# Low parts of the weights, channel sums of the convolution and the last two operations of the attention's output: from VectorE to GpSimd

## The chip, the core and the metric

The kernel runs on one core of one Trainium2 chip. The core has TensorE (PE, matrix products and transposes, into PSUM), VectorE (DVE) and ScalarE (ACT) for elementwise work, GpSimd (POOL), and SyncE (SP), which issues the DMA transfers. Each engine works through a queue of its own in a fixed order and waits on semaphores where it needs another's result. The metric is the device time of one execution in microseconds, and lower is better.

## What is computed

One layer of a streaming encoder on x of 1 x 2048 x 1024 in float32: an input norm, then nine projections of width 1024, two parallel branches (stick-breaking attention with 16 heads of 64, and a causal depthwise convolution of 31 taps with a norm over the channels), gates, a merge, an output projection and a post-norm.

```python
def _hybrid_layer(x, w_in, w_sb_proj, conv_w, conv_b, conv_ln_g, conv_ln_b, w_cv_proj, w_out, ln_g, ln_b):
    h = x @ w_in
    q, k, v, z_sb, c_val, c_gate, z_cv, g_sb, g_cv = jnp.split(h, SPLIT_POINTS, axis=-1)
    o_sb = _stick_breaking_attention(to_heads(q), to_heads(k), to_heads(v)).reshape(bsz, seq, SB_WIDTH)
    y_sb = (o_sb * jax.nn.silu(z_sb)) @ w_sb_proj
    u = c_val * jax.nn.sigmoid(c_gate)
    u = _causal_depthwise_conv(u, conv_w, conv_b)
    u = jax.nn.silu(_layer_norm(u, conv_ln_g, conv_ln_b))
    y_cv = (u * jax.nn.silu(z_cv)) @ w_cv_proj
    merged = jax.nn.sigmoid(g_sb) * y_sb + jax.nn.sigmoid(g_cv) * y_cv
    return _layer_norm(DEEPNORM_ALPHA * x + merged @ w_out, ln_g, ln_b)

# attention: A[t,s] = sigmoid(l_ts) * prod_{s<j<t} (1 - sigmoid(l_tj)), l_ts = q_t.k_s / sqrt(Dh), s < t
```

## The kernel before

**Tiling.** The sequence is turned round in time and cut into four chunks of 512 rows (`CH`), two halves of two chunks; the 1024 channels are cut into eight blocks of 128. Every float32 product runs as three passes over an exact split of both sides into a high and a low part: high x high, high x low, low x high. `split` (line 112) makes the two parts: ScalarE writes the high part as a rounded copy (L113), VectorE subtracts it from the source (L114). L114 is a helper's line: it serves the weights (`wlo`), the activations (`xl`), the transposed attention products (`tl`) and q, k, v (`st`), which the tile names tell apart.

**Projections.** A block is 128 columns of a weight against two chunks, eight pieces of six matmuls of 512 columns (L194, into a PSUM tile `mm`, of which there are two). `load_w` (line 141) brings a block's weights in two halves of 128 x 512: a DMA into `wraw` (two buffers, L148), then `split` into `whi` and `wlo` (two buffers of a whole block each). The load of the next block stands after the second piece of the present one. There are 176 blocks.

**Attention.** For a head and 256 queries, TensorE forms logits (`lg`, L572 and L573), ScalarE takes the sigmoid (`nb`, L575), VectorE runs a product along the keys (the scan on L578, over up to 1024 columns), TensorE transposes the result (`tp`, L601), `split` makes `th` and `tl`, and TensorE multiplies with differences of v (`pv`, L617). `done` (line 626) closes a chunk of a pair of heads: L631 adds the two halves into `og`; for the second head of the pair two DMAs bring v and the gate into tiles `st`, L637 adds v, L638 multiplies with the gate, and a DMA stores `og` in DRAM as `asb`. The branch projection later reads `asb` back.

**Convolution.** `conv` (line 388) runs per block of channels and half, with 46 taps (L402) on VectorE, in two rows `y0` (in the tile `cu`) and `y1` (`cy`). Each is stored, and added to `ysum` (tile `ys`): L422 for the first block, L424 for the others. `conv_mean` multiplies `ysum` with ones on TensorE once all eight blocks of the half are in. The taps are spread out by `slow_step`, at low priority.

**Order.** TensorE's order is written out by hand: two streams, attention and projections, are woven by costs in units of TensorE time, so that what one waits for is covered by the other. The queues of the other engines and of SyncE are filled by a scheduler that places each instruction where it reckons that it can start, by priority; evictions of PSUM, `tl` and `done` have a raised priority, the taps a lowered one. Buffers of `st` (seven) rotate over all users.

Of the kernel before, what the change touches and what calls it, by code (L numbers as in the profile page):

```python
# [26 lines left out]
# The weave: buffers of weights, the lead of the logits, and distances and paces in pieces of the projection stream.  # L27
# [27 lines left out]
def layer_kernel(ctx: ExitStack, tc, x, w_in, w_sb, w_cv, w_out, vecs, cw, rows, out):  # L55
    """All sequences are reversed in time: row r is position S-1-r, so that a query r reads
    the keys s > r and the stick is broken in the direction of growing s.

    Every float32 product runs as float32r passes over an exact split a = hi + lo.

    The tensor engine runs in the order of emission: two streams, the attention and the
    projections, are woven so that what one waits for is covered by the other."""
# [29 lines left out]
    def dma(dst, src):  # L92
        """A copy of bytes: float32r has float32's bits."""
        nc.sync.dma_start(out=dst.bitcast(F32) if dst.dtype == F32R else dst,
                          in_=src.bitcast(F32) if src.dtype == F32R else src)
# [16 lines left out]
    def split(src, hi, lo):  # L112
        nc.scalar.activation(hi, src, AF.Copy)  # L113
        nc.vector.tensor_tensor(out=lo, in0=src, in1=hi.bitcast(F32), op=ALU.subtract)  # L114

    def negmean(mr):
        """-mean * rstd"""
# [22 lines left out]
    # -------------------------------------------------------------- projections, in pieces  # L140
    def load_w(src, col):
        """A block of 128 columns of a weight, [block, partition, kb, column], as hi and lo, contraction on the partitions."""
        hi = wp.tile([P, KB, P], F32R, name="whi", bufs=2)
        lo = wp.tile([P, KB, P], F32R, name="wlo", bufs=2)
        for g in range(2):
# [3 lines left out]
            split(raw, hi[:, ks], lo[:, ks])  # L149
        return hi, lo  # L150

    class Fill:
        """The pieces of the projection stream: (cost in us of the tensor engine, emit)."""
# [21 lines left out]
        def parts(self, src, col, xs, use, *by):  # L175
            """A block: the pieces, per chunk, of out^T[col.., chunk] for each (chunk, acts) of xs; use(chunk, psum, ..) takes
            it, with what the loads `by` have brought. Also the item that loads the weights of the next block."""
# [43 lines left out]
        def pair(self, one, two, first=(), freed=((), ())):  # L221
            """Two blocks, the first chunk of both before the second of either. The items `first` run beside these
            pieces, freed[n] as the activations of chunk n are used up."""
# [28 lines left out]
    def prep(c):  # L252
        """The normed input of chunk c, transposed and split, into xt[c], in pieces."""
# [721 lines left out]
```

## Time and profile before

| | |
|---|---|
| time, median of 3 runs | 3037.64 us |
| the runs | 3036.8, 3037.64, 3038.7 us |
| span of the profiled execution, first to last instruction | 3036.5 us |
| mean granted TensorE clock | 0.996 |
| DMA, mean over the span | 150 GB/s |

The time of a run contains a little around the span; the runs lie 0.3 to 2.2 us above the profiled span. Busy times are sums of an engine's instructions, so a share of 97% says that the engine has nearly always something in it, not that it is at its peak. A row of groups gives the line, the engine, the operation, the tile written and the tiles read, the shape and the count, then busy time and the mean of one in ns, then the time for which the engine stood idle just before these, and what ended it. A row of waits names who waited for whom, the total in us, how often, and the longest. A row of the timeline gives the start and the duration in us.

### The profile page before, as it was taken

What the parts mean: (1) busy time and instruction counts of PE and PEld (TensorE: products, weight loads), DVE (VectorE), ACT (ScalarE), POOL (GpSimd) and SP (SyncE); (2) the same over time, 40 slices, a digit from 0 to 9 for tenths busy, and PEclk for the clock granted to TensorE, in tenths of its full rate; (3) what the DMA queues carried; (4) which work ended last, traced back from release to release, by engine and by line L of the source; (5) the groups of instructions that cost most, each with busy time, mean ns of one, the idle gap of its engine ahead of it and who ended that gap; (6) DMA issues with size and microseconds to landing.
All of it is one profiled execution on the core that took longest, in us unless ns stands there. A gap on an engine that the chain in (4) does not pass through costs nothing.

```text
span 3036.5 us, 41850 instructions
## 1 busy us (share of the span) xinstructions
PE 2959.8 (97%) x15304; PEld 2484.1 (82%) x15304; DVE 2381.6 (78%) x3175; ACT 1269.5 (42%) x2308; POOL 88.3 (3%) x178
## 2 busy tenths in 40 slices
PE   7999999999999999999999999999999999999998
PEld 6888888888887788888888888887888878878886
DVE  5587787777879888788879888879887788856656
ACT  5333333333336344444445444445445455533222
POOL 1000000000000000000000000000000000000000
PEclk9999999999999999999999999999999999999999
DMA  7543443434434533343335344335545666685552
GB/s 269 172 144 112 148 139 117 149 125 130 139 101 140 169 100 110 114 131 123 111 112 189 103 143 141 99 103 175 164 155 161 191 224 191 208 280 197 161 189 78
DMA packets 260221, 455.92 MB, mean 150 GB/s; under 512 B 30384, under 2 KB 55088, under 8 KB 259888
## 3 DMA queue, kind: packets, MB, share of 16 engines
q1 hardware_dynamic: 260016, 453.25, 46.0%
q8 instruction: 120, 1.97, 0.3%
q14 instruction: 85, 0.70, 0.1%
HBM read 292.70 MB, written 160.43 MB: 149 GB/s over the span
## 4 chain that ended last, share of the span: by engine, by line
PE 73%; DVE 11%; issue 10%; DMA 3%; ACT 2%; POOL 1%; SPq 0%; DVEq 0%; POOLq 0%; ACTq 0%
PE mm L194 52%; PE pv L617 7%; PE tp L601 6%; DVE nb L578 3%; PE lg L573 3%; PE lg L572 3%; DVE tl L114 2%; DVE wlo L114 1%; DVE cy L402 1%; PE mo L900 1%; DMA st<-ydq 1%; DMA ydq<-st 1%; DVE xl L114 1%; DVE st L494 0%; DVE st L493 0%
## 5 line engine op out<-in xcount | busy, mean ns | idle before, releaser
L194 PE MATMUL mm<-xh,whi 128*128 128x512 f32 x2816 | 1144.5, 406 | 1.7 <-ACT whi L113 1.5
L194 PE MATMUL mm<-xh,wlo 128*128 128x512 f32 x2816 | 1110.1, 394 | 1.4 <-DVE wlo L114 1.4
L194 PE MATMUL mm<-xl,whi 128*128 128x512 f32 x2816 | 1106.2, 393 | 1.2 <-DVE xl L114 1.2
L194 PEld LDWEIGHTS mm<-xh,wlo 128*128 128x128 f32 x2816 | 530.0, 188 | 120.9 <-DVE wlo L114 1.9
L194 PEld LDWEIGHTS mm<-xl,whi 128*128 128x128 f32 x2816 | 532.9, 189 | 86.8 <-DVE xl L114 2.4
L194 PEld LDWEIGHTS mm<-xh,whi 128*128 128x128 f32 x2816 | 531.5, 189 | 86.4 <-ACT whi L113 1.9
L113 ACT ACTIVATE th<-tp 128x512 fp32r<-128x512 f32 (+1 forms) x576 | 329.4, 572 | 613.9 <-PE tp L601 606.1
L114 DVE TENSOR_TENSOR tl<-tp,th 128x512 fp32r<-128x512 f32 (+1 forms) x576 | 376.5, 654 | 180.1 <-ACT th L113 178.2
L575 ACT ACTIVATE nb<-lg 128x512 f32<-128x512 f32 (+3 forms) x640 | 334.9, 532 | 308.9 <-PE lg L573 299.0
L578 DVE TENSOR_TENSOR_SCAN nb<-nb,dd 128x256 f32<-128x256 f32 (+7 forms) x256 | 345.1, 1350 | 42.2 <-ACT nb L575 41.5
L601 PE MATMUL tp<-ident,nb 128*128 128x128 f32 x2176 | 337.8, 274 | 20.3 <-DVE nb L578 18.2
L578 DVE TENSOR_TENSOR_SCAN nb<-nb,zero 128x1024 f32<-128x1024 f32 x128 | 300.0, 2346 | 36.5 <-ACT nb L575 36.2
L601 PEld LDWEIGHTS tp<-ident,nb 128*128 128x128 f32 x2176 | 263.4, 140 | 77.9 <-DVE nb L578 22.5
L113 ACT ACTIVATE whi<-wraw 128x512 fp32r<-128x512 f32 x352 | 217.6, 629 | 261.1 <-PE mm L194 238.8
L617 PE MATMUL pv<-tl,v 128*128 128x256 f32 (+1 forms) x1152 | 292.1, 282 | 12.2 <-DVE tl L114 11.6
L114 DVE TENSOR_TENSOR wlo<-wraw,whi 128x512 fp32r<-128x512 f32 x352 | 237.4, 682 | 80.0 <-ACT whi L113 52.9
L617 PE MATMUL pv<-th,v 128*128 128x256 f32 (+1 forms) x1152 | 299.5, 281 | 0.0
L572 PE MATMUL lg<-k,qd 128*128 128x512 f32 (+3 forms) x640 | 246.4, 386 | 11.6 <-ACT nb L575 7.0
L617 PEld LDWEIGHTS pv<-tl,v 128*128 128x128 f32 x1152 | 218.1, 189 | 36.4 <-DVE tl L114 17.2
L573 PE MATMUL lg<-k,ql 128*128 128x512 f32 (+3 forms) x640 | 233.7, 366 | 0.0
L617 PEld LDWEIGHTS pv<-th,v 128*128 128x128 f32 x1152 | 217.8, 189 | 18.5 <-issue 0.2
L402 DVE SCALAR_TENSOR_TENSOR cy<-cu,csum,cy 128x512 f32<-128x512 f32 x240 | 178.1, 742 | 4.4 <-ACT cy L398 0.9
(107 smaller groups left out, 2460.0 us busy)
## 6 DMA issues: line engine op xcount, KB each, us to landing
wraw<-in_w_in SPq DMA_DIRECT2D x288, 256.0 KB, 3.2
k<-kdr SPq DMA_DIRECT2D x192, 128.0 KB, 2.9
v<-vdr SPq DMA_DIRECT2D x96, 256.0 KB, 3.5
kdr<-st SPq DMA_DIRECT2D x64, 256.0 KB, 2.1
qdr<-st SPq DMA_DIRECT2D x64, 256.0 KB, 2.2
qd<-qdr SPq DMA_DIRECT2D x128, 128.0 KB, 2.8
vdr<-st SPq DMA_DIRECT2D x64, 256.0 KB, 2.0
xr<-in_x SPq DMA_DIRECT2D x32, 256.0 KB, 3.8
```

The lines of the kernel that those rows point to most:

```text
L113: nc.scalar.activation(hi, src, AF.Copy)
L114: nc.vector.tensor_tensor(out=lo, in0=src, in1=hi.bitcast(F32), op=ALU.subtract)
L194: nc.tensor.matmul(box["ps"], lhsT=l[:, kb], rhs=r[kb], start=(kb == 0 and n == 0), stop=(kb == KB - 1 and n == 2))
L402: nc.vector.scalar_tensor_tensor(out=dst, in0=src[:, j:j + HN], scalar=t, in1=first, op0=ALU.mult, op1=ALU.add)
L572: nc.tensor.matmul(lg[:, :w], lhsT=qd[c][:, js], rhs=k2[kc][:, ko:ko + w], start=True, stop=False)
L573: nc.tensor.matmul(lg[:, :w], lhsT=ql[c][:, js], rhs=k2[kc][:, ko:ko + w], start=False, stop=True)
L575: nc.scalar.activation(nb[:, o:o + w], lg[:, :w], AF.Sigmoid, scale=-QS)
L578: nc.vector.tensor_tensor_scan(out=nb[:, :w], data0=nb[:, :w], data1=dd[:, :w] if diag else zero.to_broadcast([P, w]), initial=0.0 if diag ...
L601: nc.tensor.transpose(out=tp[:, at_:at_ + P], in_=tiles[j][:, so:so + P], identity=ident)
L617: nc.tensor.matmul(o[:, :w], lhsT=lv, rhs=tt[:, o0:o0 + w], start=(diag and t == 0 and n == 0 and e == 0), stop=(last and t == nt - 1 and ...
L900: nc.tensor.matmul(ps, lhsT=a[kb][:, js], rhs=b[:, kb, qs], start=(kb == 0 and n == 0), stop=(kb == KB - 1 and n == 2))
```

## The change

`split` takes an engine for the low part, VectorE where none is given; `load_w` gives it GpSimd, so that `wlo` is formed there. The four `ysum` operations of each block of channels move to GpSimd (L422, L424), as do L637 and L638 in `done`. The high parts, all other splits, the DMAs and all shapes stay. The rest of the file's differences are comments and docstrings that are taken out; line numbers don't move.

```diff
-    def split(src, hi, lo):
+    def split(src, hi, lo, eng=None):
         nc.scalar.activation(hi, src, AF.Copy)
-        nc.vector.tensor_tensor(out=lo, in0=src, in1=hi.bitcast(F32), op=ALU.subtract)
+        (eng or nc.vector).tensor_tensor(out=lo, in0=src, in1=hi.bitcast(F32), op=ALU.subtract)
...
             raw = wp.tile([P, 4, P], F32, name="wraw", bufs=2)
             nc.sync.dma_start(out=raw, in_=src[col // P][:, ks])
-            split(raw, hi[:, ks], lo[:, ks])
+            split(raw, hi[:, ks], lo[:, ks], nc.gpsimd)
...
             for e, y in enumerate((y0, y1)):
                 dma(ydr[h, m][:, e], y)
                 if m == 0:
-                    nc.vector.tensor_copy(out=ysum[h][:, e], in_=y)
+                    nc.gpsimd.tensor_copy(out=ysum[h][:, e], in_=y)
                 else:
-                    nc.vector.tensor_tensor(out=ysum[h][:, e], in0=ysum[h][:, e], in1=y, op=ALU.add)
+                    nc.gpsimd.tensor_tensor(out=ysum[h][:, e], in0=ysum[h][:, e], in1=y, op=ALU.add)
                 yield
...
-            nc.vector.tensor_tensor(out=g, in0=g, in1=v, op=ALU.add)
-            nc.vector.tensor_tensor(out=g, in0=g, in1=z, op=ALU.mult)
+            nc.gpsimd.tensor_tensor(out=g, in0=g, in1=v, op=ALU.add)
+            nc.gpsimd.tensor_tensor(out=g, in0=g, in1=z, op=ALU.mult)
             dma(asb[c, i], g)
```

TensorE's order stays the same, instruction for instruction. On VectorE, GpSimd and SyncE the scheduler places the work anew. VectorE first, in the second half of the attention: the scans (L578, listed here as SCALAR_TENSOR_TENSOR on `nb`) over 768 and 640 columns of one step, before.

```order
L114 TENSOR_TENSOR tl<-tp,th 128x512
L114 TENSOR_TENSOR wlo<-wraw,whi 128x512
L344 TENSOR_TENSOR st<-mm,st 128x512
L578 SCALAR_TENSOR_TENSOR nb<-nb,dd 128x768
L114 TENSOR_TENSOR wlo<-wraw,whi 128x512
L402 SCALAR_TENSOR_TENSOR cy<-cu,csum,cy 128x512
L114 TENSOR_TENSOR tl<-tp,th 128x512
L402 SCALAR_TENSOR_TENSOR cy<-cu,csum,cy 128x512
L114 TENSOR_TENSOR tl<-tp,th 128x512
L578 SCALAR_TENSOR_TENSOR nb<-nb,dd 128x640
```

The same place on VectorE now:

```order
L114 TENSOR_TENSOR tl<-tp,th 128x512
L344 TENSOR_TENSOR st<-mm,st 128x512
L578 SCALAR_TENSOR_TENSOR nb<-nb,dd 128x768
L402 SCALAR_TENSOR_TENSOR cy<-cu,csum,cy 128x512
L114 TENSOR_TENSOR tl<-tp,th 128x512
L402 SCALAR_TENSOR_TENSOR cy<-cu,csum,cy 128x512
L114 TENSOR_TENSOR tl<-tp,th 128x512
L578 SCALAR_TENSOR_TENSOR nb<-nb,dd 128x640
```

Both `wlo` are gone from between the scans and the `tl`; the rest stands as it stood. GpSimd's queue in the same part of the program, where one operation on a column (L324, on `vnext`) followed the last with nothing between, before:

```order
L324 TENSOR_TENSOR st<-vnext,st 128x1
L373 COPY cu<-halo 128x2x15
L324 TENSOR_TENSOR st<-vnext,st 128x1
L326 COPY vnext<-st 128x1
L324 TENSOR_TENSOR st<-vnext,st 128x1
```

And now, from one such pair to the next:

```order
L324 TENSOR_TENSOR st<-vnext,st 128x1
L114 TENSOR_TENSOR wlo<-wraw,whi 128x512 x3
L637 TENSOR_TENSOR og<-og,st 128x512
L638 TENSOR_TENSOR og<-og,st 128x512
L114 TENSOR_TENSOR wlo<-wraw,whi 128x512 x6
L637 TENSOR_TENSOR og<-og,st 128x512
L638 TENSOR_TENSOR og<-og,st 128x512
L114 TENSOR_TENSOR wlo<-wraw,whi 128x512 x2
L124 TENSOR_TENSOR var<-var,mhalf 128x4
L114 TENSOR_TENSOR wlo<-wraw,whi 128x512 x2
L424 TENSOR_TENSOR ys<-ys,cu 128x512
L114 TENSOR_TENSOR wlo<-wraw,whi 128x512 x4
```

The low parts, the channel sums and the attention's last two operations now stand in one queue, in which each waits for the one ahead. On SyncE the loads of raw weights (L148) wait for a `wlo` on GpSimd now; the order there is changed in places, mostly by one row or two.

## Prediction

> **What bounds the kernel now.** I read the page's first two parts, then the waits of TensorE by stage, then the VectorE groups that the change moves.
>
> ```profile
> PE 2959.8 (97%) x15304; PEld 2484.1 (82%) x15304; DVE 2381.6 (78%) x3175; ACT 1269.5 (42%) x2308; POOL 88.3 (3%) x178
> ...
> PE   7999999999999999999999999999999999999998
> ```
>
> TensorE (PE) is busy 97% of the span, at nine tenths or more in all slices but the first and the last. Its idle time is 3036.5 - 2959.8 = 76.7 us, and that is the most that any change away from TensorE can win. VectorE (DVE) is busy 78%, GpSimd (POOL) 3%. The change takes work from the second and gives it to the third, so what counts is the part of the 76.7 us in which TensorE waits for VectorE, and whether that part shrinks. The next fence has the busy time by stage (first number the stage's length, then each engine), then TensorE's larger waits for VectorE in the same three stages, in us, times and longest.
>
> ```profile
> 40.00:940.00 900.00, 892.79 (x4532) 748.48 (x4531) 681.72 (x961) 339.39 (x650) 34.97 (x63) 1.00 0.43 140
> 940.00:2200.00 1260.00, 1235.24 (x6656) 1043.43 (x6655) 1059.91 (x1332) 563.21 (x1049) 22.24 (x34) 1.00 0.40 130
> 2200.00:2660.00 460.00, 442.83 (x2425) 376.35 (x2426) 382.62 (x476) 230.51 (x419) 2.03 (x2) 0.99 0.59 188
> ...
> PE tp L331 <- DVE st L320: 1.1, 1, 1.1
> ...
> PE pv L617 <- DVE tl L114: 7.8, 8, 1.9
> PE tp L601 <- DVE nb L578: 5.8, 7, 1.8
> ...
> PE tp L601 <- DVE tl L114: 1.9, 5, 0.6
> PE tp L331 <- DVE st L320: 1.8, 1, 1.8
> ...
> PE tp L601 <- DVE nb L578: 12.3, 7, 3.2
> PE pv L617 <- DVE tl L114: 3.9, 5, 1.4
> ```
>
> The third number is VectorE's load: 681.72 / 900 = 75.7%, 1059.91 / 1260 = 84.1% and 382.62 / 460 = 83.2%. The waits are 1.1 us (0.12% of the stage), then 7.8 + 5.8 + 1.9 + 1.8 = 17.3 us (1.37%), then 12.3 + 3.9 = 16.2 us (3.5%). Two things follow. The prize is about **34.6 us**, 1.1% of the kernel. And it is all but absent where VectorE is at 76% and there where it is at 83 to 84%, so a few points of VectorE's load matter. This is how such a wait looks:
>
> ```profile
> 1282.73 0.66 DVE L114 TENSOR_TENSOR wlo<-wraw,whi 128x512 fp32r<-128x512 f32 x1
> ...
> 1283.31 0.74 DVE L402 SCALAR_TENSOR_TENSOR cy<-cu,csum,cy 128x512 f32<-128x512 f32 x1
> ...
> 1283.97 0.68 DVE L114 TENSOR_TENSOR tl<-tp,th 128x512 fp32r<-128x512 f32 x1
> ...
> 1284.71 0.38 PE L617 MATMUL pv<-tl,v 128*128 128x256 f32 x1 [1.90 <-DVE tl L114]
> ```
>
> TensorE stood 1.90 us for a `tl` that stood on VectorE behind a weight's low part (`wlo`) and a tap of the convolution. Without the `wlo` it is some 0.6 us earlier.
>
> **What is taken off VectorE.** Groups of VectorE by shape: busy time, mean ns of one, then its idle time before them.
>
> ```profile
> L114 DVE TENSOR_TENSOR wlo<-wraw,whi 128x512 fp32r<-128x512 f32 x352 | 237.4, 682 | 80.0 <-ACT whi L113 52.9 <-PE tp L601 17.7 <-PE lg L573 7.9
> L637 DVE TENSOR_TENSOR og<-og,st 128x512 f32<-128x512 f32 x32 | 22.0, 686 | 17.5 <-DMA st<-vtd 17.4
> L638 DVE TENSOR_TENSOR og<-og,st 128x512 f32<-128x512 f32 x32 | 21.8, 680 | 1.7 <-DMA st<-gat_5b 0.7 <-DMA st<-gat_3b 0.5 <-DMA st<-gat_4b 0.2
> L424 DVE TENSOR_TENSOR ys<-ys,cy 128x512 f32<-128x512 f32 x14 | 9.5, 679 | 0.0
> L424 DVE TENSOR_TENSOR ys<-ys,cu 128x512 f32<-128x512 f32 x14 | 9.5, 678 | 0.0
> ```
>
> That is 237.4 + 22.0 + 21.8 + 9.5 + 9.5 = **300.2 us** in 444 instructions, 12.6% of VectorE's busy time (the four copies that begin a sum are left out as too small). Up to 80.0 + 17.5 + 1.7 = 99 us go too in which VectorE stood at the head of its queue for ScalarE's `whi` or for a load. I don't count them: what stood behind may not have been ready either.
>
> **What GpSimd pays.** No row shows a two-input operation of this size there. The nearest are a memset of twice the columns and a two-input operation on one column (fastest, median, slowest):
>
> ```profile
> L506 POOL MEMSET dd<- 128x1024 f32 x1 | 1.0, 952 | 0.0
> ...
> L324 POOL TENSOR_TENSOR st<-vnext,st x24: 191/692/1798, 63.3 to 2010.3; 128x1 f32<-128x1 f32 x24
> ```
>
> One pass over 512 columns is 0.952 / 2 = 0.48 us, the fixed part 0.19 us. One pass gives 0.67 us, three passes (two reads and a write in turn) 1.63 us; I take two reads in turn, 0.19 + 0.95 = 1.14 us, between them. 444 x 1.14 = 506 us (297 to 724), so GpSimd goes from 3% to about 20%. It isn't short of time. The Trainium skill (GPSIMD Engine Reference, Elementwise — side-by-side cycle accounting) puts such an operation at about 2.6 cycles an element at 1.2 GHz, from which an estimate is 1.11 us and a sum of 493 us; no run here shows it.
>
> Does a slower low part make TensorE wait? The 352 halves are 176 blocks in 3036.5 us, 17.3 us each. A block's weights are loaded when two of the eight pieces of the block before are through, so six eighths of a block, 12.9 us, cover the load, `whi` and `wlo`. GpSimd's 0.5 us more for each half lies under that, and so do a few us of waiting in its queue. The present cover shows in the one wait, at 2679 us:
>
> ```profile
> PE mm L194 <- DVE wlo L114: 1.4, 1, 1.4
> ...
> SPq L148 <- DVE wlo L114: 458.9, 232, 14.8
> ```
>
> There the attention ends, its last sums (L637, L638) go to the store and come back at once, and they now stand in GpSimd's queue ahead of urgent low parts: I add 2 us (0 to 5). The second row is the other queue: SyncE (SP) issues the load of the next raw weights as soon as the low part has freed the buffer, and stands there 232 times; what is queued behind it (stores that free the seven `st` buffers, loads of keys) is later by what the low part is later. These have leads of several us, so I put it at 1 us, from 0 to 10.
>
> **What the two engines do to each other.** This decides it. GpSimd's few operations are stretched at times; each pair below is a GpSimd row and what VectorE ran beside it.
>
> ```profile
> 1544.58 2.21 POOL L373 COPY cu<-halo 128x30 f32<-128x30 f32 x1 [2.40 <-DVE ys L424]
> ...
> 1544.44 2.34 DVE L578 TENSOR_TENSOR_SCAN nb<-nb,zero 128x1024 f32<-128x1024 f32 x1
> 1546.70 0.66 DVE L424 TENSOR_TENSOR ys<-ys,cy 128x512 f32<-128x512 f32 x1
> ...
> 342.73 1.50 POOL L322 TENSOR_SCALAR st<-st 128x1 f32<-128x1 f32 x1 [77.17 <-DMA ql<-qdr]
> ...
> 342.93 0.68 DVE L320 TENSOR_TENSOR st<-st 128x511 f32<-128x511 f32 x1
> 343.53 0.68 DVE L578 TENSOR_TENSOR_SCAN nb<-nb,dd 128x256 f32<-128x256 f32 x1
> ...
> 121.81 0.18 POOL L326 COPY vnext<-st 128x1 f32<-128x1 f32 x1
> ...
> 121.62 0.68 DVE L114 TENSOR_TENSOR tl<-tp,th 128x512 fp32r<-128x512 f32 x1
> ```
>
> A copy of 30 columns took 2.21 us and ended at 1546.79, as the scan beside it did (1546.78). An operation on one column took 1.50 us and ended at 344.23, after two VectorE operations back to back (the last ended at 344.21). Beside `tl`, which has one input in PSUM, a copy took 0.18 us. So GpSimd stands while VectorE runs an operation with both inputs in SBUF. The Trainium skill (SBUF — State Buffer, SBUF: two separate sides) says that the two share a port pair as an exclusive lock, that a VectorE operation with two SBUF inputs takes it against a GpSimd operation that reads SBUF, and that whichever starts first keeps it for the whole instruction. The trace agrees for GpSimd's side; that VectorE stands for GpSimd, no row shows, since GpSimd's operations here were too short.
>
> By what part of its time VectorE is exposed:
>
> ```profile
> L578 DVE TENSOR_TENSOR_SCAN nb<-nb,dd 128x256 f32<-128x256 f32 (+7 forms) x256 | 345.1, 1350 | 42.2 <-ACT nb L575 41.5
> ...
> L578 DVE TENSOR_TENSOR_SCAN nb<-nb,zero 128x1024 f32<-128x1024 f32 x128 | 300.0, 2346 | 36.5 <-ACT nb L575 36.2
> ...
> L402 DVE SCALAR_TENSOR_TENSOR cy<-cu,csum,cy 128x512 f32<-128x512 f32 x240 | 178.1, 742 | 4.4 <-ACT cy L398 0.9 <-issue 0.3
> L402 DVE SCALAR_TENSOR_TENSOR cu<-cd,cwt,cu 128x512 f32<-128x512 f32 x240 | 178.1, 742 | 2.7
> L402 DVE SCALAR_TENSOR_TENSOR cy<-cu,cwt,cy 128x512 f32<-128x512 f32 x240 | 178.0, 742 | 2.3
> ```
>
> Scans and taps alone are 300.0 + 345.1 + 3 x 178.1 = 1179 us, half of VectorE's busy time, all with both inputs in SBUF. If GpSimd holds off VectorE in turn, each of the 444 operations costs VectorE between nothing and the whole 1.14 us. About half the time the next VectorE operation is of the exposed kind; then it waits 1.14 us if it is next at once, and 1.14 - 0.68 = 0.46 us if a `tl` of 0.68 us lies between. Half and half, that is 0.5 x 0.8 = 0.40 us each, **178 us** in all (0 to 506).
>
> **The sum.** VectorE: -300 + 178 = -122 us, 5.1% of its time, or 4.3 points of load in the two late stages. By the line through the first and second stage (1.25 points of waiting for 8.4 of load) the second loses 0.64% of 1260 us, 8 us; by that through the first and third (3.4 for 7.5) the third loses 1.9% of 460 us, 9 us: 17 us together. A more cautious count: the 34.6 us are some 34 waits; with 4 us of queue ahead of each, 5.1% of it is 0.2 us, 7 us together. I take 11 us, between the two, and give back 2 us at 2679 us and 1 us on SP's queue: **-8 us**. The span of 3036.5 us becomes 3028.5; the runs of before lie 0.3 to 2.2 us above the span and their median 1.1, so the forecast is **3030 us**, 0.25% below the 3037.6.
>
> Ends: with nothing held off, VectorE loses 12.6% of its load and all 34.6 us go, 3003. With 1.14 us each, VectorE gains 506 - 300 = 206 us, 8.6% or 7 points: the same lines give +14, +15 and +9 us in the three stages, 3037.6 + 38 = 3076.
>
> **Rivals.** (1) *VectorE stands for GpSimd, and longer than it is relieved.* One mechanism: a GpSimd operation holds off scan or tap, the `tl` and `nb` behind it come late, TensorE stands. It turns the sign once the mean hold is above 300 / 444 = 0.68 us; at 0.9 us the load rises by 100 us, 3.5 points, and the lines give +18 us, 3056; at the end above 3076. For it: half of VectorE's time is of the exposed kind, and in the rows above GpSimd enters as soon as such an operation ends. Against: VectorE's next operation began at 1546.70, before the scan's end, without a gap for the copy's sake. The Trainium skill (Perfetto Trace Analysis, Optimizing Scalar/DVE Operations) warns that the shared port may make a move between these two worthless. 24%.
> (2) *No change.* The waits for `nb` (5.8 + 12.3 us) mostly follow a scan of 2.35 us that had only just got its input; taking work from ahead of it helps little, and GpSimd's holds give the rest back: 3037, from 3032 to 3043. For it: in the example only 0.66 of the last 2.1 us ahead of the matmul are moved. 30%.
> (3) *The change moves the work, but its lateness is what counts*: SP stands longer at the raw weights' loads, the `st` buffers come free late, and the evictions of `mm` hold TensorE. 352 loads later by 1 us with a tenth of it uncovered are 35 us, less the 11 us gained: 3062. Against: TensorE waited for low parts once. 4%.
> The forecast, faster: 42%.
>
> **How the numbers follow.** Faster by over 0.2% (6 us, about what a measurement of this kernel can tell from no change) is the forecast's 42%; within it is rival 2's 30%; slower is 24% and 4%. Both signs hold much of it, so: the forecast's own range is 3008 to 3031, and the range for 8 in 10 is 3010 to 3068, which leaves out the last of the full relief and the worst of the holds.
>
> **What would show it.** Right: VectorE at about 2080 us less its stretched operations, GpSimd near 600 us or more, TensorE's waits for `tl` and `nb` below 34.6 us, none for `wlo` outside 2660 to 2690 us. Rival 1 shows as taps above 742 ns and scans above 2346 ns, and more waits for `tl` and `nb`; rival 3 as waits for `wlo` and longer waits of SP at L148. A GpSimd mean above 2 us, or TensorE's waits for VectorE unchanged with VectorE's load well down, would make the forecast wrong.

## The result: slower by 1.5%, and the profile after

The changed kernel takes **3083.5 us** (median of 4 runs, 3081.8 to 3084.7) against 3038.2 us before (3036.8 to 3039.1): a ratio of 1.0148, 95% interval 1.0133 to 1.0162. The prediction said 3030, with a range up to 3068. The profiled execution's span went from 3036.5 to 3081.1 us, 44.6 us more. First the page's busy times after:

```profile
PE 2976.3 (97%) x15304; PEld 2491.8 (81%) x15304; DVE 2314.3 (75%) x2727; ACT 1271.1 (41%) x2308; POOL 766.2 (25%) x626
```

VectorE (DVE) did get lighter, from 2381.6 to 2314.3 us and from 78 to 75% of its time. TensorE (PE) still stands longer: 3081.1 - 2976.3 = 104.8 us idle, against 76.7. It is also 16.5 us longer busy with the same 15304 instructions. The same three stages as in the prediction (the stage's length, then each engine's busy time, then TensorE's granted clock), and below them, stage by stage, what TensorE waited for:

```profile
40.00:940.00 900.00, 889.03 (x4504) 744.32 (x4502) 648.64 (x788) 336.68 (x644) 273.83 (x228) 1.00 0.42 138
940.00:2200.00 1260.00, 1223.98 (x6547) 1032.50 (x6547) 1017.54 (x1132) 557.56 (x1034) 313.02 (x219) 0.99 0.39 126
2200.00:2660.00 460.00, 433.44 (x2364) 366.30 (x2363) 365.41 (x400) 224.76 (x412) 85.37 (x57) 0.99 0.57 184
```

```profile
PE tp L331 <- DVE st L320: 1.9, 1, 1.9
PE tp L601 <- DVE tl L114: 1.6, 2, 1.3
PE tp L601 <- DVE nb L578: 1.1, 2, 0.9
...
PE tp L601 <- DVE nb L578: 11.9, 8, 3.5
PE pv L617 <- DVE tl L114: 9.5, 11, 1.9
...
PE tp L601 <- DVE tl L114: 4.9, 5, 1.8
...
PE tp L601 <- DVE nb L578: 10.5, 6, 3.6
PE pv L617 <- DVE tl L114: 9.8, 10, 2.3
```

VectorE's load is 648.64 / 900 = 72.1%, 1017.54 / 1260 = 80.8% and 365.41 / 460 = 79.4%: in every stage three to four points below before. The waits shown are 4.6 us, 26.3 us and 20.3 us, where before had 1.1, 17.3 and 16.2. So load and waits went in opposite directions. Over the whole span TensorE's waits of more than 0.15 us grew by 20.3 us for VectorE, by 5.7 us for ScalarE and by 1.6 us for GpSimd, nearly all of the 28.1 us of idle time. The groups show what became of the operations (busy time, mean ns of one, idle time before):

```profile
L578 DVE TENSOR_TENSOR_SCAN nb<-nb,zero 128x1024 f32<-128x1024 f32 x128 | 311.6, 2437 | 45.3 <-ACT nb L575 45.0
L402 DVE SCALAR_TENSOR_TENSOR cy<-cu,cwt,cy 128x512 f32<-128x512 f32 x240 | 209.0, 871 | 2.2
L402 DVE SCALAR_TENSOR_TENSOR cu<-cd,cwt,cu 128x512 f32<-128x512 f32 x240 | 206.7, 861 | 2.8
...
L701 DVE TENSOR_TENSOR st<-mm,gt 128x512 f32<-128x512 f32 x64 | 43.9, 686 | 84.0 <-PE mm L194 78.4 <-DMA gt<-gat_3s 5.2
L631 DVE TENSOR_TENSOR og<-pv,st 64x512 f32<-64x512 f32 x64 | 43.8, 685 | 25.3 <-ACT st L630 24.1
...
L638 POOL TENSOR_TENSOR og<-og,st 128x512 f32<-128x512 f32 x32 | 59.0, 1843 | 2.4 <-PE mm L194 0.2
...
L637 POOL TENSOR_TENSOR og<-og,st 128x512 f32<-128x512 f32 x32 | 47.7, 1492 | 232.7 <-DMA st<-vtd 155.3 <-DVE og L631 49.8 <-DVE bs L262 13.6
```

The taps (L402) went from 742 to 861 and 871 ns, the scans on 1024 columns from 2346 to 2437. L701 and L631, which have one input in PSUM, kept their 686 and 685 ns (the same two figures before). GpSimd's own times for a low part (count: fastest, median, slowest ns):

```profile
L114 POOL TENSOR_TENSOR wlo<-wraw,whi x352: 1265/1299/3278, 13.2 to 2961.8; 128x512 fp32r<-128x512 f32 x176
```

So an undisturbed low part takes 1.27 to 1.30 us there. The slow ones are those in which GpSimd stood for VectorE: of the 122 above 1.45 us, 117 began while a VectorE operation with no input in PSUM was running, of the other 230 only 25. The other direction shows as plainly: after the first 40 us, 245 VectorE operations took over 0.15 us longer than the median of their like before, and within 0.1 us of the start of every one of them a GpSimd operation was running, though GpSimd is busy only a quarter of the time. One place shows how this reaches TensorE. The timeline of the kernel after, rows of GpSimd, VectorE and TensorE (start us, duration us; in brackets the wait):

```profile
1645.57 2.97 POOL L114 TENSOR_TENSOR wlo<-wraw,whi 128x512 fp32r<-128x512 f32 x2 [13.45 <-ACT whi L113]
...
1645.64 1.77 DVE L494 TENSOR_TENSOR st<-st 128x512 f32<-128x512 f32 x1
1647.34 3.08 DVE L578 TENSOR_TENSOR_SCAN nb<-nb,dd 128x896 f32<-128x896 f32 x1
...
1650.47 0.44 PE L601 MATMUL tp<-ident,nb 128*128 128x128 f32 x2 [3.50 <-DVE nb L578]
```

Two low parts ran from 1645.57 to 1648.54. L494 began beside the first and took 1.77 us in place of the 0.70 that is its mean before; the scan behind it took 3.08 in place of a mean of 2.02. That is 1.07 + 1.06 = 2.1 us of the 3.5 for which TensorE then stood. What followed is seen in the same kernel's windows around that place (length, busy TensorE, weight loads, VectorE, ScalarE, GpSimd, then TensorE's granted clock):

```profile
1646.00:1651.00 5.00, 1.50 (x11) 1.19 (x10) 5.00 (x3) 1.47 (x3) 2.54 (x2) 1.00 0.70 236
1651.00:1653.00 2.00, 0.99 (x5) 0.67 (x4) 1.96 (x5) 0.00 (x0) 0.00 (x0) 0.64 0.95 344
1653.00:1658.00 5.00, 5.00 (x16) 4.03 (x16) 4.25 (x6) 2.98 (x5) 0.00 (x0) 0.50 0.07 26
1658.00:1662.00 4.00, 4.00 (x22) 3.42 (x21) 2.38 (x5) 2.44 (x5) 0.00 (x0) 0.95 0.31 103
```

After the wait TensorE worked for some 6.8 us at a clock of 0.50, so a wait of 4.5 us (3.50 and another of 1.00) cost 3.4 us more. Over the whole kernel, the span and mean granted clock of before and of after:

```profile
core 0: 3036.5 us, clock 0.996
```

```profile
core 0: 3081.1 us, clock 0.992
```

The clock took 0.4% of 3036.5 = 12 us before and 0.8% of 3081.1 = 25 us after. Idle time (+28.1 us) and clock (+12.5 us) together make 40.6 of the 44.6 us. In windows of 1 us over the whole span I count six stretches of half clock before and eleven after. The last of each lies at the kernel's end, where TensorE has no more work; the other five and ten take 1.7 or 3.4 us each, about 12 us more after than before.

### The profile page after: what moved, and what is told of

The parts are those of the page before. It is cut to its first block, busy times and chain, and to the rows that moved or that the text cites. A ratio compares the mean times of both kernels' runs of the same rounds, so it can differ in the third digit from the quotient of the medians.

```text
span 3081.1 us, 41942 instructions
## 1 busy us (share of the span) xinstructions
PE 2976.3 (97%) x15304; PEld 2491.8 (81%) x15304; DVE 2314.3 (75%) x2727; ACT 1271.1 (41%) x2308; POOL 766.2 (25%) x626
## 5 line engine op out<-in xcount | busy, mean ns | idle before, releaser
L114 POOL TENSOR_TENSOR wlo<-wraw,whi 128x512 fp32r<-128x512 f32 x352 | 530.4, 1517 | 1605.0 <-ACT whi L113 1466.9
L578 DVE TENSOR_TENSOR_SCAN nb<-nb,dd 128x256 f32<-128x256 f32 (+7 forms) x256 | 376.6, 1474 | 61.2 <-ACT nb L575 60.6
L578 DVE TENSOR_TENSOR_SCAN nb<-nb,zero 128x1024 f32<-128x1024 f32 x128 | 311.6, 2437 | 45.3 <-ACT nb L575 45.0
L402 DVE SCALAR_TENSOR_TENSOR cy<-cu,csum,cy 128x512 f32<-128x512 f32 x240 | 204.8, 853 | 11.3 <-ACT cy L398 7.5
```

Source lines behind the costliest of these rows:

```text
L114: (eng or nc.vector).tensor_tensor(out=lo, in0=src, in1=hi.bitcast(F32), op=ALU.subtract)
L402: nc.vector.scalar_tensor_tensor(out=dst, in0=src[:, j:j + HN], scalar=t, in1=first, op0=ALU.mult, op1=ALU.add)
L578: nc.vector.tensor_tensor_scan(out=nb[:, :w], data0=nb[:, :w], data1=dd[:, :w] if diag else zero.to_broadcast([P, w]), initial=0.0 if diag ...
```

## The experiments

Fourteen kernels, each timed in three rounds (d_ys_og_only in five) beside the kernel before on the same chip. **Hold** below is how much longer VectorE was busy than it would be by its own work alone. For that, a_relief gives the measure: 444 operations less took 2381.6 - 2128.6 = 253 us off VectorE, 0.57 us each, not the 0.68 of a single row, since rows of VectorE overlap a little. **Price** is the time lost per us of hold, against before or against a_relief, whichever has the same work on VectorE. Ratios are turned into us with before's 3038.2.

| kernel | what it is | ratio to before, 95% | VectorE busy | hold | price |
|---|---|---|---|---|---|
| after | the change | 1.0148 [1.0133, 1.0162] | 2314.3 | 186 | 0.32 |
| a_relief | moved work left out | 0.9953 [0.9938, 0.9968] | 2128.6 | 0 | |
| b_price | before, and GpSimd does the moved work again | 1.0427 [1.0408, 1.0447] | 2651.9 | 270 | 0.48 |
| c_wlo_only | low parts alone moved | 1.0124 [1.0100, 1.0147] | 2334.4 | 153 | 0.32 |
| d_ys_og_only | the other 96 operations alone moved | 1.0042 [1.0030, 1.0055] | 2371.7 | 45 | 0.35 |
| e_memset | before, 704 memsets on GpSimd | 1.0002 [0.9993, 1.0011] | 2384.1 | 3 | |
| f_twice_dve | before, VectorE does the moved work again | 1.0161 [1.0147, 1.0175] | 2635.5 | 254 (own work) | 0.19 |
| l_dup_first | f with the added low parts put first | 1.0175 [1.0158, 1.0192] | 2637.8 | 256 (own work) | 0.21 |
| g_cut4 | after, low parts in four pieces | 1.0165 [1.0151, 1.0179] | 2234.3 | 106 | 0.61 |
| i_one_input | before, GpSimd operations with one input | 1.0141 [1.0125, 1.0156] | 2444.9 | 63 | 0.68 |
| j_free512 | before, 352 GpSimd operations nobody waits for | 1.0218 [1.0201, 1.0235] | 2557.5 | 176 | 0.38 |
| k_free128 | the same in 1408 short pieces | 1.0105 [1.0090, 1.0120] | 2469.7 | 88 | 0.36 |
| n_relief_hold | a_relief, 352 operations nobody waits for, one tile read twice | 1.0050 [1.0035, 1.0065] | 2227.3 | 99 | 0.30 |
| p_two_tiles | the same, two tiles read | 1.0087 [1.0072, 1.0102] | 2279.5 | 151 | 0.27 |
| q_from_raw | the same, on the raw weights | 1.0101 [1.0084, 1.0117] | 2280.8 | 152 | 0.30 |

(c and d: by 0.57 us for each moved operation; their own relief is added to the loss at a_relief's rate.) The theories at first: (1) VectorE is held off by GpSimd's operations; (2) the scheduler's new order costs; (3) what GpSimd now makes comes late.

### What the move takes away, and what it brings

a_relief: the kernel without the moved work, in the order of VectorE that this leaves.

```diff
-        lo = wp.tile([P, KB, P], F32R, name="wlo", bufs=2)
+        lo = wzero
...
-            split(raw, hi[:, ks], lo[:, ks])
+            nc.scalar.activation(hi[:, ks], raw, AF.Copy)
...
-                else:
-                    nc.vector.tensor_tensor(out=ysum[h][:, e], in0=ysum[h][:, e], in1=y, op=ALU.add)
...
-            nc.vector.tensor_tensor(out=g, in0=g, in1=v, op=ALU.add)
-            nc.vector.tensor_tensor(out=g, in0=g, in1=z, op=ALU.mult)
```

> The relief alone: the moved work is done nowhere. All low parts of the weights are one constant tile of zeros, the channel sums keep only their first block, and the attention's last two operations are left out (so the output lacks these); GpSimd has no more to do than before. Theory 1 (VectorE is held off by GpSimd's operations): nothing is held off, and VectorE's load falls by 12.6%; by the prediction's line the waits of 34.6 us in front of TensorE go, 3003 us, by its cautious count 3022 us; so 3000 to 3025 us, taps at 742 ns. Theory 2 (the scheduler's new order on VectorE and ScalarE is what costs): this kernel has nearly the same new order, so it is slow too, 3060 to 3085 us. Theory 3 (the low parts come late from GpSimd): as theory 1 here.

It took 3027.2 us, by the ratio 14 us less than before and 2 us above the range of theory 1; the taps stayed at 742 ns. Its page and its waits of TensorE:

```profile
PE 2960.0 (98%) x15304; PEld 2485.1 (82%) x15304; DVE 2128.6 (70%) x2731; ACT 1268.7 (42%) x2308; POOL 81.3 (3%) x179
```

```profile
PE tp L602 <- DVE nb L579: 14.0, 10, 2.5
...
PE pv L618 <- DVE tl L114: 7.4, 13, 1.4
```

Without the moved work TensorE still waits 14.0 us for scans and 7.4 us for `tl`. The relief was never worth 34.6 us. And 2677 of its 2731 VectorE instructions follow one another as in the kernel after: an order close to the new one isn't slow by itself, so theory 2 falls: from here to the kernel after it is 59 us the other way.

b_price: VectorE as before; GpSimd does the same operations once more, in place on buffers that are used up.

```diff
             split(raw, hi[:, ks], lo[:, ks])
+            nc.gpsimd.tensor_tensor(out=raw, in0=raw, in1=hi[:, ks].bitcast(F32), op=ALU.subtract)
...
+                nc.gpsimd.tensor_tensor(out=d0[:, :HN], in0=y, in1=y, op=ALU.add)
...
+            nc.gpsimd.tensor_tensor(out=v, in0=v, in1=z, op=ALU.add)
+            nc.gpsimd.tensor_tensor(out=z, in0=v, in1=z, op=ALU.mult)
```

> The price alone: VectorE does all that it did before, in the order of before, and GpSimd does an operation of the same size and kind beside each of the 448 moved ones, a second time, into buffers that are already read, so that nobody waits for its results except for the buffers. Theory 1: VectorE is held off as in the changed kernel, its taps take 850 to 870 ns in place of 742, and with nothing taken off VectorE the time is above that of the changed kernel, 3085 to 3130 us. Theory 2: the order is that of before, so 3035 to 3045 us. Theory 3: nothing waits for a low part from GpSimd, so 3035 to 3050 us.

3173.5 us, above the 3085 to 3130 of theory 1, with the taps at 861 ns, as expected. VectorE is 270 us longer busy with the same 3175 instructions, 0.60 us for each of the 448 operations. GpSimd's work costs VectorE time, whoever uses the result.

c_wlo_only: the change without L424, L637 and L638.

```diff
-            split(raw, hi[:, ks], lo[:, ks])
+            split(raw, hi[:, ks], lo[:, ks], nc.gpsimd)
```

> Only the low parts of the weights on GpSimd, the channel sums and the attention's last two operations on VectorE: 352 of the 448 operations. Theory 1: the price goes by the number of GpSimd's operations, 352 / 448 of the 45 us, so 3065 to 3080 us. Theory 2: anything between 3038 and 3083 us. Theory 3: the low parts are those that come late, so the whole of it, 3075 to 3085 us.

3080.6 us: most of the loss comes with the low parts. The time lies in the range of theory 3 and 0.6 us above that of theory 1, so this run doesn't tell hold from lateness.

d_ys_og_only: the rest of the change alone (the edit is the change's at L422, L424, L637 and L638).

> The change without the low parts: only the channel sums and the last two operations of the attention's output (96 operations) on GpSimd, the low parts on VectorE. With the price in proportion to the number of operations, by the kernel after (448 operations, +45 us): +10 us, 3050 us. By the difference of after (3083) and c_wlo_only (3081, low parts only): +3 us, 3043 us. If these 96 operations had stood ahead of awaited VectorE results in before: below 3036 us. Theory 3 (lateness) would show as SyncE standing longer for og and TensorE waiting for the loads behind it: 3045 us or more.

3052.6 us, +13 us, near the 10 us in proportion to the number of operations. The 96 operations cost about what the low parts cost, each. The time also lies in the range of theory 3, and its signs are there in part: SyncE stands 114.3 us for `og` in place of 76.8, and TensorE's wait for `whi` behind a load rose from 1.5 to 4.2 us (p_two_tiles below, where nothing waits for GpSimd's results, has 4.2 us as well). TensorE's waits for VectorE rose by only 2.7 us. For these 96 operations the run doesn't part hold from lateness.

e_memset: as before, and GpSimd writes the raw weights' buffer after its last reader.

```diff
             split(raw, hi[:, ks], lo[:, ks])
+            for _ in range(2):
+                nc.gpsimd.memset(raw, 0.0)
```

> All as before on VectorE, and GpSimd writes zeros twice over each raw weight buffer after it was used (704 memsets of 128x512, about 0.5 us each, so as much of GpSimd's time as the low parts take by one pass less). They read nothing. Theory 1 in the form that GpSimd's reading of SBUF is what holds VectorE off: taps stay at 742 ns, 3035 to 3045 us (the buffer is free about 1 us later). Theory 1 in the form that any GpSimd access holds it off: taps at 800 ns or more and 3060 us or more. Theories 2 and 3: 3035 to 3045 us.

3040.5 us, no difference. The taps of VectorE and the memsets in it:

```profile
L404 DVE SCALAR_TENSOR_TENSOR cy<-cu,csum,cy 128x512 f32<-128x512 f32 x240 | 178.3, 743 | 4.6 <-ACT cy L400 0.9 <-issue 0.3
...
L151 POOL MEMSET wraw<- 128x512 f32 x704 | 368.7, 527 | 2025.7 <-DVE wlo L114 1933.8 <-issue 21.0 <-ACT nb L577 15.8
```

A GpSimd that writes 128x512 704 times leaves the taps at 743 ns: it must read SBUF to hold VectorE off. These memsets also free the raw buffer about 1.05 us later, which costs nothing.

### Load or hold

Two further theories: (A) TensorE's waits follow VectorE's load, however it came about; (B) it counts where the time is lost. f_twice_dve is b_price with the added operations on VectorE itself.

```diff
             split(raw, hi[:, ks], lo[:, ks])
+            nc.vector.tensor_tensor(out=raw, in0=raw, in1=hi[:, ks].bitcast(F32), op=ALU.subtract)
...
+                nc.vector.tensor_tensor(out=d0[:, :HN], in0=y, in1=y, op=ALU.add)
...
+            nc.vector.tensor_tensor(out=v, in0=v, in1=z, op=ALU.add)
+            nc.vector.tensor_tensor(out=z, in0=v, in1=z, op=ALU.mult)
```

> The kernel before, with the work that b_price gave to GpSimd a second time (352 low parts, the channel sums, the last two operations of the attention's output) done that second time on VectorE instead. It adds about 300 us of busy time to VectorE, a little more than the 270 us by which GpSimd's operations lengthened VectorE's in b_price (3173 us). Theory A (TensorE's waits follow VectorE's total load, however the load came about): as slow as b_price or slower, 3165 to 3210 us. Theory B (what counts is where the time is lost: the scheduler puts added VectorE operations where nothing urgent stands behind them, a hold by GpSimd falls ahead of any operation): clearly below b_price, 3060 to 3120 us.

```profile
PE 2976.3 (96%) x15304; PEld 2491.5 (81%) x15304; DVE 2635.5 (85%) x3623; ACT 1269.1 (41%) x2308; POOL 85.3 (3%) x178
```

3088.4 us. VectorE is at 85%, and the kernel is about as slow as the one after with VectorE at 75%. The same work a second time costs 49 us on VectorE and 130 us on GpSimd. Theory A falls.

l_dup_first gives f's added low parts priority:

```diff
+            with tc.high_priority(offset=500):
+                nc.vector.tensor_tensor(out=raw, in0=raw, in1=hi[:, ks].bitcast(F32), op=ALU.subtract)
```

> f_twice_dve (the moved work done a second time on VectorE, 3088 us) with the 352 added low parts at a high priority, so that 216 of VectorE's 3623 rows stand elsewhere: an added low part stands directly ahead of a tl or nb 144 times in place of 115, directly ahead of a scan 73 times or so in place of 37 to 40. The work is the same. If place decides (theory B): 3095 to 3130 us, towards the price of a hold. If only the amount counts (theory A): 3083 to 3093 us.

3093.1 us; its interval overlaps f's. So the place shows no price here, but the test was a weak one: in the traces 144 of the 352 added low parts stand directly ahead of a scan or a `tl`, in place of 115. Theory B is neither shown nor refuted by 29 of them, and what sets a hold apart from work stays open.

### Length of the operations, and inputs

g_cut4:

```diff
-            split(raw, hi[:, ks], lo[:, ks], nc.gpsimd)
+            nc.scalar.activation(hi[:, ks], raw, AF.Copy)
+            for j in range(4):
+                nc.gpsimd.tensor_tensor(out=lo[:, g * 4 + j], in0=raw[:, j], in1=hi[:, g * 4 + j].bitcast(F32), op=ALU.subtract)
```

> The kernel after, with each low part on GpSimd cut into 4 operations of 128 columns (1408 for 352). If a hold of VectorE lasts as long as the GpSimd operation that makes it and its length counts (theory B): each hold is at most about 0.4 us in place of 1.3 us, and the time falls from 3083 to 3040 to 3065 us; taps that were held show +0.4 us, not +1 us. If only the total of GpSimd's time on SBUF counts (theory A): 4 fixed parts for one raise GpSimd's total, so 3083 to 3110 us. If lateness of the low parts counted (theory 3): slower than 3083 us as well, with TensorE waiting for wlo.

3089.8 us, no gain, in the range for GpSimd's total time and not in that for the length, though the hold fell from 186 to 106 us. One reason shows in its waits of TensorE:

```profile
PE tp L333 <- POOL st L326: 4.2, 4, 2.4
```

GpSimd is at 37% there, and its small urgent operations stand behind the pieces. But this row is a small part of the loss. Beside the kernel after, TensorE's waits for VectorE did fall, from 70.1 to 59.7 us, while those for ScalarE rose from 17.6 to 23.2 us and those for GpSimd from 1.6 to 4.9 us, and TensorE was 8.9 us longer busy with the same instructions. Why ScalarE comes later is not explained.

i_one_input, on GpSimd:

```diff
+            nc.gpsimd.tensor_scalar(out=raw, in0=raw, scalar1=2.0, scalar2=None, op0=ALU.mult)
...
+                nc.gpsimd.tensor_scalar(out=d0[:, :HN], in0=y, scalar1=2.0, scalar2=None, op0=ALU.mult)
...
+            nc.gpsimd.tensor_scalar(out=v, in0=v, scalar1=2.0, scalar2=None, op0=ALU.mult)
+            nc.gpsimd.tensor_scalar(out=z, in0=z, scalar1=2.0, scalar2=None, op0=ALU.mult)
```

> The kernel before and, on GpSimd, 448 operations of 128x512 with ONE input in SBUF and an output in SBUF (a multiplication by 2 in place on the raw weights, and on buffers of the convolution and the attention's output that are used up), in the places of b_price's two-input operations. If any GpSimd operation that reads SBUF holds VectorE off: taps at 780 to 850 ns in place of 743, time 3060 to 3173 us. If it takes two inputs on GpSimd's side: taps at 743 ns and time 3040 us, as with the memsets. Per unit of GpSimd's time the same hold as in b_price (270 us for 717 us) would make the ratio of VectorE's gain to GpSimd's gain 0.38 again.

3083.1 us, the taps at 768 to 776 ns: one input read from SBUF is enough for a hold, though a smaller one (63 us). That is 0.08 us for each of the 789 us that GpSimd gained, where b_price's 0.38 was expected, and the taps lie below the expected 780 to 850 ns; why is open. Its price of 0.68 is out of line. As in b_price, the raw buffer comes free only after VectorE's low part and then GpSimd's operation; what of the two prices is due to that was not separated.

j_free512 and k_free128 take that away: nothing waits for their operations.

```diff
+    scr = wp.tile([P, 4, P], mybir.dt.bfloat16, name="scr", bufs=1)
...
+            nc.gpsimd.tensor_tensor(out=scr, in0=hi[:, ks].bitcast(F32), in1=hi[:, ks].bitcast(F32), op=ALU.add)
```

k_free128 has four such operations of 128 columns, into a float32 tile.

> The kernel before, untouched on VectorE, and on GpSimd 352 operations of 128x512 with two inputs in SBUF, which read a weight's high part twice and write a scratch tile that nothing reads. Nothing waits for them (the high part is kept for a whole block anyway), so neither the weight's loads nor any result of the kernel come later. If the hold of VectorE alone makes the loss: VectorE's busy time rises by 180 to 230 us (352 operations at 0.52 to 0.60 us, the means of the kernel after and of b_price), and the time by 80 to 110 us, 352/448 of b_price's 133 us: 3120 to 3150 us. If b_price's loss came from the raw weights' buffers being free later: 3040 to 3060 us.

> The same with 1408 operations of 128x128 in place of 352 of 128x512 (0.45 us each alone in g_cut4, against 1.27 us), nothing waiting for them. If the length of a single hold counts more than their sum: VectorE's busy time +100 to +150 us, the time clearly below that of the run with 352 operations, 3060 to 3090 us, and so g_cut4's lack of a gain was the lateness of GpSimd's small operations behind a busier queue. If the time goes with GpSimd's time on SBUF: 1408 x 0.45 = 634 us against 352 x 1.27 = 447 us, so slower than the run with 352 operations, by up to 40%.

3106.0 us, below the expected 3120 to 3150, and 3070.8 us, as expected. A hold that delays nothing else costs 0.38 and 0.36 us per us; in j_free512 VectorE's 3175 instructions stand in the very order of before. Where the hold falls is not as in the change, though: about half of j_free512's, 89 us, lies on VectorE's own low parts (682 ns before), which start beside GpSimd's operation.

```profile
L114 DVE TENSOR_TENSOR wlo<-wraw,whi 128x512 fp32r<-128x512 f32 x352 | 326.7, 936 | 69.9 <-ACT whi L113 57.5 <-PE tp L604 4.7 <-DMA k<-kdr 3.8
```

Short operations hold VectorE off less in all (88 us against 176), though GpSimd's own busy time is longer. So for the hold, four short operations beat a long one; g_cut4 lost that again.

### Hold or lateness

The last question was whether the hold alone makes the loss, or late low parts and late weight buffers do. Three kernels on top of a_relief (the moved work is left out in all): n_relief_hold reads the high part twice, p_two_tiles the zero tile and the high part, q_from_raw the raw weights and the high part.

```diff
+            nc.gpsimd.tensor_tensor(out=scr, in0=hi[:, ks].bitcast(F32), in1=hi[:, ks].bitcast(F32), op=ALU.add)
...
+            nc.gpsimd.tensor_tensor(out=scr, in0=wzero[:, ks].bitcast(F32), in1=hi[:, ks].bitcast(F32), op=ALU.subtract)
...
+            nc.gpsimd.tensor_tensor(out=scr, in0=raw, in1=hi[:, ks].bitcast(F32), op=ALU.subtract)
```

> The kernel a_relief (the moved operations done nowhere: low parts a constant zero tile, channel sums of the first block alone, the last two operations of the attention's output left out; 3027 us) and on GpSimd 352 operations of 128x512 that read a weight's high part twice and write a scratch tile that nothing reads: the hold of the change's low parts without any result that could come late. If hold and relief make the whole result: VectorE's busy time 170 to 200 us above a_relief's 2129, time 3065 to 3085 us, as in c_wlo_only (3081). If half or more of the loss was that low parts or weight buffers come later: 3035 to 3055 us.

n_relief_hold's 3053.2 us lie in the range for lateness, but it doesn't decide: its operations were shorter (median 1042 ns) and held VectorE off for 99 us, not 170 to 200.

```profile
L150 POOL TENSOR_TENSOR scr<-whi x352: 1035/1042/2904, 14.2 to 2934.9; 128x512 f32<-128x512 f32 x176
```

> n_relief_hold with two different tiles as GpSimd's operands (the constant zero tile and the weight's high part, into a scratch tile), so that an operation should take the 1.27 to 1.30 us of the change's low parts and not 1.04; as in a_relief the moved operations are done nowhere. Nothing waits for it. At 0.30 us of time for each us of hold (the kernel after against a_relief: 56 us for 186): if the hold of VectorE comes back to 170 to 190 us, 3075 to 3085 us, and the hold alone makes the loss. If the hold is back and the time stays at 3050 to 3060 us, the rest is lateness. If the hold stays near 100 us, the operations' length is not what set it, and 3050 to 3060 us.

> The same with the raw weights and the high part as GpSimd's operands, the change's own, into a scratch tile: the raw weights' buffer comes free as late as in the kernel after, no low part is waited for (they are a constant zero tile; the other moved operations are left out, as in a_relief). If the hold alone counts: as p_two_tiles, within 5 us, and 3075 to 3085 us. If the raw buffer's lateness counts: 15 us or more above p_two_tiles. If the low part's own lateness counts: more than 15 us below c_wlo_only's 3081 us.

```profile
L150 POOL TENSOR_TENSOR scr<-wlo,whi x352: 1261/1299/3145, 14.0 to 2946.9; 128x512 f32<-128x512 f32 x176
```

```profile
PE 2969.6 (97%) x15304; PEld 2489.2 (81%) x15304; DVE 2279.5 (74%) x2731; ACT 1268.5 (41%) x2308; POOL 606.4 (20%) x531
```

With the change's own 1.30 us, the hold is 151 and 152 us and the times are 3066.7 and 3070.8 us, 8 and 4 us below the lower end of what I expected, with a hold that is 20 to 40 us smaller than expected. By the ratios p_two_tiles lies 41 us above a_relief and q_from_raw 45 us. The 4 us between them are what a late raw buffer could cost; the intervals overlap. Add the other 96 operations, d_ys_og_only's 13 us and the 3 us that their relief would have brought at a_relief's rate: 45 + 13 + 3 = 61 us, and the kernel after lies 59 us above a_relief. So the hold explains the result, within intervals of some 5 us either way for each of these times; low parts that come late have no share that these runs can show. Of the 59 us, 45 are shown with nothing but the hold and a late raw buffer; for the 16 us of the other 96 operations, lateness of `og` isn't ruled out.

No kernel here that computes the same is faster than the one before. a_relief's 14 us are what taking this work off VectorE brought with nothing put elsewhere, and no run found a place for it that costs less.

## Why the prediction was wrong

**What held.** TensorE is the bound and the sign hangs on what GpSimd does to VectorE: so it was. *"If GpSimd holds off VectorE in turn"*: it does. The hold was put at 0.40 us for each operation, 178 us in all; it was 186 us for 448, 0.41 each. Half of 444 operations were to hold VectorE off by 0.8 us, and 245 VectorE operations were stretched, by 0.80 us in the mean. That it came so close is in part luck: for operations of the same size it was 0.28 us each in n_relief_hold and 0.60 us in b_price. The signs named for rival 1 all came, slower taps and scans and more waits for `tl` and `nb`. The rule on the shared port that the prediction took from the Trainium skill (SBUF — State Buffer, SBUF: two separate sides) is now seen from the other side too: taps are stretched from 742 to 861 ns and more, scans of 1024 columns from 2346 to 2437, `tl` with its PSUM input keeps its mean of 654, and beside memsets the taps stay at 743. Lateness of low parts was put at 2 us; TensorE waited once, 0.5 us. GpSimd's price was put at 1.14 us and is 1.27 to 1.30 alone and 1.52 in the mean; the estimate from the Trainium skill (GPSIMD Engine Reference, Elementwise — side-by-side cycle accounting), 1.11 us, was as low. Neither matters to the time, since GpSimd has room.

**The step that failed** is in the sum: *"VectorE: -300 + 178 = -122 us"*, turned into waits *"by the line through the first and second stage"*. It takes a us of hold as equal to a us of VectorE's work and lets waits follow the load. Both terms were priced wrong.

1. The relief. VectorE's busy time fell by 253 us without the moved work, not by 300.2 (rows overlap), and all of it brought 14 us, where the lines of load gave the whole 34.6: 14 / 253 = 0.06 us per us. The prediction's own cautious count comes close when it is applied to the full relief: 34 waits, 4 us of queue ahead of each, 10.6% of it, 14 us.
2. The hold. 186 us cost 59 us, 0.32 each, five times as much; in kernels where nothing waits for GpSimd it was 0.27 to 0.38. So -14 + 59 = **+45 us**, what was measured. (The 59 us are taken from the same two times; what checks them is the 61 us from p_two_tiles, q_from_raw and d_ys_og_only.) VectorE's net load does fall, by 67 us, and tells nothing.
3. The clock. Every term of the sum counted waits alone. About 12 of the 45 us are TensorE at half clock after a long wait.

The lines of load aren't far off for work that is added on VectorE itself: f_twice_dve's 254 us are 10.7% of its load, 46 us by these lines, and 49 us were measured. About a third of those 49 is TensorE's longer busy time at the lower clock (16.5 us), which the lines leave out, so this nearness is partly luck too. What the lines miss is that the relief brings less than half of what they give it, and that a hold isn't work. (At the prediction's upper end the 14, 15 and 9 us belong to the second, third and first stage; their sum stands.)

**Rival 1** had the mechanism and the place, with 24%, but by the same sum its turning point was a mean hold of 0.68 us. With the measured prices it is 14 us / (448 x 0.32) = 0.10 us: 0.41 is far beyond it. That such time is dear and the relief cheap was not in any row of before.

**Why a hold is dearer than work** is shown in part. In the traces I counted, after 40 us, TensorE's waits of 0.4 us or more for VectorE, and VectorE operations over 0.15 us longer than the median of their like before. In the kernel after, 245 operations are stretched, by 0.8 us in the mean and 1.15 at most. Of 40 waits (54.6 us), 32 (44.8 us) have more than 0.5 us of stretch in operations that ended within the 6 us before the wait's end; a random moment has that in 33% of cases. The other 8 waits make 9.8 us. Before, there were 28 waits with 34.2 us, and a_relief has 18 with 20.8 us. So relief does take away waits, and holds make more of them. Why VectorE's own added work costs less than a hold, 0.19 to 0.21 us per us against 0.27 to 0.38, stays open: l_dup_first moved too few operations to tell whether it is their place in the order. That a hold comes when GpSimd happens to be ready, and no order can be made for it, is my guess and was not tried.

## What to carry to other kernels

When work is moved to an engine whose operations may hold off those of the one it left, price the two directions apart: what the relieved engine's work costs the bound engine (leave the work out and look), and what the other engine's operations cost while nothing waits for them. Busy time of an engine off the critical path is no measure for either: here it fell and the kernel lost 45 us. And where the bound is TensorE, add to each wait of about two us or more the half clock that may follow it.

## What the runs showed of the hardware

- **TensorE's clock after a wait.** Stretches at 0.50 last about 3.4 or 6.8 us and follow waits from about 1.8 us on, though not all: a wait of 2.26 us at 2503 us in the kernel after was followed by one, one of 2.97 us at 2646 us was not. b_price has nineteen of them and a mean clock of 0.985. The Trainium skill (TensorE: Matmul & The Clock Gate, Part 1: The HAM clock gate) tells of a free-running window of about 3.4 us and half clock after an idle one; the lengths agree, and the traces add that a wait shorter than the window can be enough.
- **GpSimd's operations of 128x512.** Two tiles 1.30 us, the same tile twice 1.04, one tile times a number 1.50, and 128 columns of two tiles 0.46 (medians). From 1.30 and 0.46: 2.2 ns a column and 0.18 us fixed. By the prediction's count of passes over SBUF one input would have been cheaper than two.
- **A short GpSimd operation holds VectorE off far less than in proportion**: in k_free128 0.06 us for one of 128 columns (88 / 1408), in j_free512 0.50 us for one of 512 (176 / 352). The scratch tiles of these two differ in type; with the change's own operands, less d_ys_og_only's 45 us, it is 0.04 us in g_cut4 ((106 - 45) / 1408) and 0.40 us in the kernel after ((186 - 45) / 352).
